# Five of nine gates and four adaLN vectors written between the blocks of an attention, in step with their size

## The chip, the cores and the metric

One core of one Trainium2 chip. The number is device time in microseconds (us) for one launch; lower is better. TensorE (PE) multiplies, with its weight loads shown as a row of their own (PEld); VectorE is DVE, ScalarE is ACT, GpSimd is POOL, SyncE is SP. SP and ACT issue most DMAs, POOL a few.

## What is computed

One layer of a hybrid decoder on 1024 prompt rows and 8 x 4 new rows (1056 columns in all, held transposed):

```
mod = silu(c) @ w_ada + b_ada                 # six vectors of 1024: sh1 sc1 g1 sh2 sc2 g2
h   = rmsnorm(x) * (1 + sc1) + sh1
z   = h @ w_in + b_in                         # q, k, v, forget, glu, gate_a, gate_b
o   = fox_attention(q, k, v, logf)            # 8 heads of 64, causal, with a forget bias
y_a = o @ w_pa
y_b = silu(layernorm(conv(glu))) @ w_pb + b_pb
x   = x + g1 * ((sigmoid(gate_a) * y_a + sigmoid(gate_b) * y_b) @ w_o)
x   = x + g2 * (swiglu(rmsnorm(x) * (1 + sc2) + sh2))
```

Arithmetic is float32 made of two float32r halves, so each product is three matmuls (high by high, high by low, low by high).

## The kernel before

The kernel is written as one long program, and a planner then orders it: it steps through a simulation of the chip, and whenever an engine is free it takes the earliest-written instruction that is ready in that simulation. Each engine executes the resulting list strictly in that order. `in_order(x)` adds one constraint: x may not be placed ahead of the instruction written just before it on the same engine. `tc.high_priority()` moves a block forward in the planner's ranking.

A **gate** (`gate_steps(i)`) is one 128-row slice of gate_a (i = 0 to 7) or gate_b (8 to 15) before its sigmoid: it loads a 512 KB weight tile on SP (L309, buffer tag `wr`, three buffers), splits it in high and low halves (ACT L315, POOL L318), and multiplies it with three column chunks of 384, 384 and 288, eight steps (k) of three matmuls (`mm3`, L327 to L329) each. After each chunk ACT copies the result out of PSUM (L486) and stores it in `gD`. The products take PSUM buffers of tag `mm`, of which there are two while the attention runs.

An **adaLN vector** (`ada(i)`) is one of the six slices of `mod`. It streams eight 512 KB tiles of `w_ada` through the same `wr` buffers (SP, L157), each used by four matmuls of 32 rows (L161) into one `mm` buffer; then come an ACT copy, two transposes (L170) and one DVE addition (L173). Vectors 2 to 5 are not needed before the layer's output products.

The **attention** has 32 units: head h by column block c2, in the order 3, 1, 2, 0 for each head. `scores` makes two blocks of 128 softmax rows: matmuls L815, L817, L818 into PSUM, DVE L820 to add the bias and find the minimum, DVE L825, ACT L826 for the exponential, DVE L827 and DVE or ACT for the division. `weighted` runs up to two units later: transposes L874, split into halves by ACT L876 and DVE L877, products with V L886 and L887, sum of two halves by ACT L897 and DVE L898, store from the ACT queue. `load_head` brings five operands of a head from HBM on SP (L849 to L853), two heads ahead. `conv_ln` (three times) normalises the convolution branch in between. Before the attention stand the gates 15 to 10; behind it, in the written order, gates 9, 8, 6, 5, 4, 3, 2, 1, 0, with the vectors 2 to 5 behind the gates 6, 5, 4 and 3. The planner takes these for the places where TensorE would be free during the attention. Then follow the convolution's product (`branch(1, ...)`, loads `yr` L941), gate 7, and the rest of the layer.

```
for n, u in enumerate(units):
    ready.append((*u, scores(*u)))
    if n in (0, 8, 16):
        conv_ln(n // 8)
    if len(ready) > 2:
        weighted(*ready.pop(0))
    if n % 4 == 1 and 4 < n < 28:
        load_head(n // 4 + 1)
for x in ready:
    weighted(*x)
for i in (9, 8, 6, 5, 4, 3, 2, 1, 0):
    gate(i, pool, sp)
    if 3 <= i < 7:
        ada(8 - i, wp, "wr", 3, ps_mm)
```

Of the kernel before, what the change touches and what calls it, by code (L numbers as in the profile page):

```python
# [29 lines left out]
KD = D // P  # L30
# [14 lines left out]
ON = 150  # L45
KS = 2
NHR = 8
HF = 2
UW = KL + NP + DB * (KL + DT)

# [36 lines left out]
def hybrid_step(ctx, tc, xT, cT, vec, bvf, con, stT, ptab, ptabr, kcT, vc, lfc, w_ada, w_in, w_vfa, w_vfb,  # L87
# [61 lines left out]
    act.activation(cTt, cTt, AF.Silu)  # L149
    wap = mkpool(name="wap", bufs=1, side="right")  # L150

    def ada(i, pl, tag, bufs, psum):

        ps = psum()
        for k in range(KD):
            w = pl.tile([P, KD, P], F32, name="wa", tag=tag, bufs=bufs).rearrange("p a b -> p (a b)")
            d = sp.dma_start(w, w_ada[k * P:(k + 1) * P, i * 1024:(i + 1) * 1024])  # L157
            if i < 2:
                in_order(d)
            for g in range(4):  # L160
                pe.matmul(ps[32 * g:32 * g + 32, :256], cTt[:, k, :], w[:, g * 256:(g + 1) * 256],  # L161
                          start=(k == 0), stop=(k == KD - 1))
        with tc.high_priority() if i < 2 else nullcontext():
            s = ev(wp, "gev", 4)
            d = act.copy(s[:, :256], ps[:, :256])
            if i == 1:
                in_order(d)
            pt = psum()
            for q in range(2):
                pe.transpose(pt[:, q * P:(q + 1) * P], s[:, q * P:(q + 1) * P], ident)  # L170
            src = pt[:, :256].rearrange("p (q g r) -> p g q r", q=2, g=4)[:, :, :, 0:9]
            b = V[:, V_ADA + i * 8:V_ADA + i * 8 + 8].rearrange("p (g q) -> p g q", g=4)
            dve.tensor_tensor(mod[:, i * 8:(i + 1) * 8, :].rearrange("p (g q) r -> p g q r", g=4),  # L173
                              src, b.unsqueeze(3).broadcast_to([P, 4, 2, 9]), OP.add)
            if i == 1:
                gains(0, V_RMS1, 8)

    def gains(i, vcol, sc):
        g = V[:, vcol:vcol + KD]
# [142 lines left out]
        with tc.high_priority():  # L322
            return split_w(*args, **kw)

    def mm3(ps, w, k, nk, xh, xl, n):
        wh, wl = w
        pe.matmul(ps[:, :n], wh[:, k, :], xh, start=(k == 0), stop=False)  # L327
        pe.matmul(ps[:, :n], wh[:, k, :], xl, start=False, stop=False)  # L328
        pe.matmul(ps[:, :n], wl[:, k, :], xh, start=False, stop=(k == nk - 1))  # L329

# [138 lines left out]

    gD = [[dram.tile([P, T], F32, name=f"gD{w}_{j}") for j in range(KD)] for w in range(2)]  # L470

    def gate_steps(i, *wq):

        which, j = divmod(i, KD)
        w = w_in_tile(16 + i, *wq)
        for c in range(3):
            o, n = CH[c]
            ps = ps_mm()
            ah, al = A[c]
            for k in range(KD):  # L480
                mm3(ps, w, k, KD, ah[:, k, :n], al[:, k, :n], n)
                if k < KD - 1:
                    yield
            t = ev(wp, "gev", 4)
            vcol = (V_BGA, V_BGB)[which] + j
            act.activation(t[:, :n], ps[:, :n], AF.Identity, bias=V[:, vcol:vcol + 1])  # L486
            act.dma_start(gD[which][j][:, o:o + n], t[:, :n])
            yield
# [410 lines left out]
        act.dma_start(oD[p][64 * h2:64 * h2 + 64, c2 * 256:(c2 + 1) * 256], ot)  # L899

    units = [(h, c2) for h in range(H) for c2 in (3, 1, 2, 0)]
    ready = []
    load_head(0)
    load_head(1)
    for n, u in enumerate(units):
        ready.append((*u, scores(*u)))
        if n in (0, 8, 16):
            conv_ln(n // 8)
        if len(ready) > 2:
            weighted(*ready.pop(0))  # L910
        if n % 4 == 1 and 4 < n < 28:
            load_head(n // 4 + 1)
    for x in ready:
        weighted(*x)
    for i in (9, 8, 6, 5, 4, 3, 2, 1, 0):
        gate(i, pool, sp)
        if 3 <= i < 7:
            ada(8 - i, wp, "wr", 3, ps_mm)
    gains(1, V_RMS2, 32)
    atl.release()  # L920
    atp.release()
# [487 lines left out]
```

## Time and profile before

| what | value |
|---|---|
| median of 3 runs | 1625.02 us (1624.96 to 1627.49) |
| the profiled execution | 1624.47 us, span of its instructions 1622.7 us |
| PE busy | 1562.2 us, 96% |
| PEld busy | 1474.2 us, 91% |
| DVE busy | 1060.4 us, 65% |
| ACT busy | 698.6 us, 43% |
| mean granted clock of TensorE | 0.989 |

Matmuls overlap in the records, so PE counts as busy as long as one is in flight; the weight loads beside it (PEld) thin out where the matmuls come less densely. The attention runs from about 406 to 671 us.

### The profile page before, as it was taken

To read this page: it belongs to the slowest core of one execution; us is meant where nothing else is said; L and a number is where in the kernel's file an instruction comes from. 1 tells how busy PE (TensorE), PEld (TensorE's weight loads), DVE (VectorE), ACT (ScalarE), POOL (GpSimd) and SP (SyncE) were. 2 spreads that over 40 slices of the span, in tenths; PEclk is the share of its full clock that TensorE was granted. 3 is DMA by queue.
4 is the path that set the end of the run, shared out by engine and by line. 5 is a ranking of instruction groups with operands and counts; after the bars stand their busy time and mean duration, and the time that the engine had idled before them with its cause. 6 is when DMAs were issued, how large, how long until landed. Compare 5 with 4: busy or idle time off the path is not lost.

```text
span 1622.7 us, 29627 instructions
## 1 busy us (share of the span) xinstructions
PE 1562.2 (96%) x11280; PEld 1474.2 (91%) x11280; DVE 1060.4 (65%) x2206; ACT 698.6 (43%) x1398; POOL 131.9 (8%) x102
## 2 busy tenths in 40 slices
PE   5999999999998989999999999999999999999997
PEld 3899978778977878999999999999999999999997
DVE  6943379999797867256659995555555596225644
ACT  4552212121376766444427653333333375224342
POOL 2121022341220101000000000000000000000000
PEclk9999999999999999999999999999999999999998
DMA  9196475877697774454554322222222257334552
GB/s 370 57 311 183 150 222 181 255 227 220 196 248 227 208 212 155 141 169 144 181 184 132 118 93 86 80 80 79 80 80 80 79 186 256 115 89 136 192 173 82
DMA packets 141424, 261.86 MB, mean 161 GB/s; under 512 B 24634, under 2 KB 81594, under 8 KB 140642
## 3 DMA queue, kind: packets, MB, share of 16 engines
q1 hardware_dynamic: 102802, 209.37, 41.4%
q10 hardware_dynamic: 36384, 43.01, 7.6%
q0 software_dynamic: 2096, 7.60, 1.5%
q8 instruction: 88, 1.44, 0.4%
q14 instruction: 54, 0.44, 0.1%
HBM read 206.44 MB, written 53.48 MB: 160 GB/s over the span
## 4 chain that ended last, share of the span: by engine, by line
PE 77%; DVE 11%; DMA 6%; ACT 2%; POOL 2%; issue 2%; SPq 1%; ACTq 0%; DVEq 0%; POOLq 0%
PE mm L1177 25%; PE mm L1278 16%; PE mm L329 8%; PE mm L327 8%; PE mm L328 8%; DVE acc L528 5%; DMA wa<-w_ada 2%; PE ptr L874 2%; POOL wl L318 1%; PE mm L561 1%; PE mm L560 1%; PE mm L562 1%; PE mm L161 1%; PE ppv L887 1%; PE ppv L886 1%
## 5 line engine op out<-in xcount | busy, mean ns | idle before, releaser
L327 PE MATMUL mm<-ah,wh 128*128 128x384 f32 (+2 forms) x768 | 252.0, 329 | 7.6 <-ACT ah L291 3.7
L1278 PE MATMUL mm<-f,wo 128*128 128x352 f32 x1584 | 256.8, 323 | 0.0
L1278 PEld LDWEIGHTS mm<-f,wo 128*128 128x128 f32 x1584 | 254.8, 188 | 0.0
L329 PE MATMUL mm<-ah,wl 128*128 128x384 f32 (+2 forms) x768 | 251.3, 328 | 2.6 <-POOL wl L318 2.6
L328 PE MATMUL mm<-al,wh 128*128 128x384 f32 (+2 forms) x768 | 251.8, 328 | 0.0
L1177 PE MATMUL mm<-c,wc 128*128 128x264 f32 x1776 | 235.7, 285 | 1.0 <-ACT wc L1134 0.5
L1177 PE MATMUL mm<-b,wc 128*128 128x264 f32 x1680 | 227.3, 286 | 3.5 <-DVE wc L1135 1.3
L1177 PEld LDWEIGHTS mm<-c,wc 128*128 128x128 f32 x1776 | 224.2, 188 | 2.0 <-ACT gev L1182 0.9
L1177 PEld LDWEIGHTS mm<-b,wc 128*128 128x128 f32 x1680 | 213.9, 189 | 5.1 <-ACT wc L1134 1.8
L528 DVE SCALAR_TENSOR_TENSOR acc<-u,vec,acc 128x1024 f32<-128x1024 f32 x120 | 171.4, 1450 | 1.2
L327 PEld LDWEIGHTS mm<-ah,wh 128*128 128x128 f32 x768 | 145.5, 190 | 17.1 <-issue 5.9
L328 PEld LDWEIGHTS mm<-al,wh 128*128 128x128 f32 x768 | 145.3, 189 | 11.3 <-issue 10.5
L1229 DVE TENSOR_TENSOR wo<-wr,wo 128x512 fp32r<-128x512 f32 x108 | 69.7, 647 | 129.9 <-ACT wo L1228 129.3
L329 PEld LDWEIGHTS mm<-ah,wl 128*128 128x128 f32 x768 | 145.5, 190 | 7.3 <-POOL wl L318 3.5
L1134 ACT CAST wc<-wr 128x512 fp32r<-128x512 f32 x144 | 88.6, 620 | 138.8 <-PE mm L1177 131.0
L1228 ACT CAST wo<-wr 128x512 fp32r<-128x512 f32 x108 | 63.2, 585 | 151.0 <-PE mm L1278 143.8
L1135 DVE TENSOR_TENSOR wc<-wr,wc 128x512 fp32r<-128x512 f32 x144 | 98.7, 691 | 35.6 <-ACT wc L1134 34.4
L318 POOL TENSOR_TENSOR wl<-wr,wh 128x1024 fp32r<-128x1024 f32 x27 | 87.6, 3249 | 319.7 <-ACT wh L315 280.3
L315 ACT CAST wh<-wr 128x1024 fp32r<-128x1024 f32 (+1 forms) x64 | 59.8, 940 | 91.0 <-PE mm L328 45.9
L327 PE MATMUL mm<-b,wh 128*128 128x264 f32 x256 | 72.7, 285 | 0.5 <-ACT wh L315 0.5
L329 PE MATMUL mm<-b,wl 128*128 128x264 f32 x256 | 72.1, 285 | 0.6 <-DVE wl L318 0.6
L328 PE MATMUL mm<-b,wh 128*128 128x264 f32 x256 | 72.4, 283 | 0.0
(293 smaller groups left out, 2665.4 us busy)
## 6 DMA issues: line engine op xcount, KB each, us to landing
wr<-w_fi SPq DMA_DIRECT2D x52, 512.0 KB
wa<-w_ada SPq DMA_DIRECT2D x48, 512.0 KB
wr<-w_fo SPq DMA_DIRECT2D x36, 512.0 KB
kt<-kcT SPq DMA_DIRECT2D x64, 256.0 KB
vt<-vc SPq DMA_DIRECT2D x64, 256.0 KB
hD<-h ACTq DMA_DIRECT2D x44, 264.0 KB
wr<-w_in SPq DMA_DIRECT2D x18, 512.0 KB
wr<-w_o SPq DMA_DIRECT2D x16, 512.0 KB
```

The lines of the kernel that those rows point to most:

```text
L315: d = act.copy(wh[:, r, :], raw[:, r, :])
L318: eng.tensor_tensor(wl[:, r, :], raw[:, r, :], wh[:, r, :].bitcast(F32), OP.subtract)
L327: pe.matmul(ps[:, :n], wh[:, k, :], xh, start=(k == 0), stop=False)
L328: pe.matmul(ps[:, :n], wh[:, k, :], xl, start=False, stop=False)
L329: pe.matmul(ps[:, :n], wl[:, k, :], xh, start=False, stop=(k == nk - 1))
L528: dve.scalar_tensor_tensor(a[:, :NP], u[:, j:j + NP], wv[:, j:j + 1], a[:, :NP], op0=OP.mult, op1=OP.add)
L1134: act.copy(w[:, 0, :n], raw)
L1135: dve.tensor_tensor(w[:, 1, :n], raw, w[:, 0, :n].bitcast(F32), OP.subtract)
L1177: pe.matmul(ps[:, :HS], w[i][:, r, k * P:(k + 1) * P], x[s][:, k, :], start=(new and k == 0 and j == 0), stop=(k == 3 and j == 2), skip_gr ...
L1228: act.copy(x[:, 0, :], raw)
L1229: dve.tensor_tensor(x[:, 1, :], raw, x[:, 0, :].bitcast(F32), OP.subtract)
L1278: pe.matmul(ps[e][:, :n], w[r][:, k * P:(k + 1) * P], f[x], start=(k0 + k + i == 0), stop=(k0 + k == HT - 1 and i == 2))
```

## The change

Gates 9, 8 and 6 are written ahead of the attention. Gates 5, 4, 3, 2, 1 and vectors 2 to 5 are cut into 136 steps (120 of one k of a gate, 16 of two tiles of a vector), which are written between the attention's blocks: after each `scores` and each `weighted`, as many as bring the share of steps written up to the share of the attention's cost written, where a block of c2 counts 4 * c2 + 3. Every quarter of the gate steps takes one vector's four steps with it, one after each of its first four fours. The first matmul of each chunk of these gates, and the second tile's matmuls of each vector step, are held behind what is written before them on TensorE. A vector's step loads two tiles and multiplies the later one first. Gate 0 is written behind the attention.

```diff
--- before.py
+++ after.py
@@ -45,6 +45,7 @@
 ON = 150
 KS = 2
 NHR = 8
+FILL = (5, 4, 3, 2, 1)
 HF = 2
 UW = KL + NP + DB * (KL + DT)
 
@@ -149,17 +150,39 @@
     act.activation(cTt, cTt, AF.Silu)
     wap = mkpool(name="wap", bufs=1, side="right")
 
-    def ada(i, pl, tag, bufs, psum):
+    def ada(*args):
+        for _ in ada_steps(*args):
+            pass
+
+    def ada_steps(i, pl, tag, bufs, psum):
 
         ps = psum()
-        for k in range(KD):
+
+        def load(k):
             w = pl.tile([P, KD, P], F32, name="wa", tag=tag, bufs=bufs).rearrange("p a b -> p (a b)")
             d = sp.dma_start(w, w_ada[k * P:(k + 1) * P, i * 1024:(i + 1) * 1024])
             if i < 2:
                 in_order(d)
+            return w
+
+        def product(k, w, first, last, pinned=False):
             for g in range(4):
-                pe.matmul(ps[32 * g:32 * g + 32, :256], cTt[:, k, :], w[:, g * 256:(g + 1) * 256],
-                          start=(k == 0), stop=(k == KD - 1))
+                mm = pe.matmul(ps[32 * g:32 * g + 32, :256], cTt[:, k, :], w[:, g * 256:(g + 1) * 256],
+                               start=first, stop=last)
+                if pinned:
+                    in_order(mm)
+
+        if i < 2:
+            for k in range(KD):
+                product(k, load(k), k == 0, k == KD - 1)
+        else:
+
+            for k in range(0, KD, 2):
+                w0, w1 = load(k), load(k + 1)
+                product(k + 1, w1, k == 0, False)
+                product(k, w0, False, k == KD - 2, True)
+                if k < KD - 2:
+                    yield
         with tc.high_priority() if i < 2 else nullcontext():
             s = ev(wp, "gev", 4)
             d = act.copy(s[:, :256], ps[:, :256])
@@ -174,6 +197,7 @@
                               src, b.unsqueeze(3).broadcast_to([P, 4, 2, 9]), OP.add)
             if i == 1:
                 gains(0, V_RMS1, 8)
+        yield
 
     def gains(i, vcol, sc):
         g = V[:, vcol:vcol + KD]
@@ -322,9 +346,11 @@
         with tc.high_priority():
             return split_w(*args, **kw)
 
-    def mm3(ps, w, k, nk, xh, xl, n):
+    def mm3(ps, w, k, nk, xh, xl, n, pinned=False):
         wh, wl = w
-        pe.matmul(ps[:, :n], wh[:, k, :], xh, start=(k == 0), stop=False)
+        first = pe.matmul(ps[:, :n], wh[:, k, :], xh, start=(k == 0), stop=False)
+        if pinned:
+            in_order(first)
         pe.matmul(ps[:, :n], wh[:, k, :], xl, start=False, stop=False)
         pe.matmul(ps[:, :n], wl[:, k, :], xh, start=False, stop=(k == nk - 1))
 
@@ -469,7 +495,8 @@
 
     gD = [[dram.tile([P, T], F32, name=f"gD{w}_{j}") for j in range(KD)] for w in range(2)]
 
-    def gate_steps(i, *wq):
+    def gate_steps(i, *wq, pinned=False):
+
 
         which, j = divmod(i, KD)
         w = w_in_tile(16 + i, *wq)
@@ -478,7 +505,7 @@
             ps = ps_mm()
             ah, al = A[c]
             for k in range(KD):
-                mm3(ps, w, k, KD, ah[:, k, :n], al[:, k, :n], n)
+                mm3(ps, w, k, KD, ah[:, k, :n], al[:, k, :n], n, pinned and k == 0)
                 if k < KD - 1:
                     yield
             t = ev(wp, "gev", 4)
@@ -899,23 +926,63 @@
         act.dma_start(oD[p][64 * h2:64 * h2 + 64, c2 * 256:(c2 + 1) * 256], ot)
 
     units = [(h, c2) for h in range(H) for c2 in (3, 1, 2, 0)]
+
+    def gate_fill():
+        for i in FILL:
+            yield from gate_steps(i, pool, sp, pinned=True)
+
+    def ada_fill():
+        for i in (2, 3, 4, 5):
+            yield from ada_steps(i, wp, "wr", 3, ps_mm)
+
+    def fillers():
+
+        gates, vectors = gate_fill(), ada_fill()
+        part = 3 * KD * len(FILL) // 4
+        for _ in range(4):
+            for n in range(part):
+                next(gates)
+                yield
+                if n % 4 == 3 and n < 16:
+                    next(vectors)
+                    yield
+        for _ in vectors:
+            pass
+
+
+    fill = fillers()
+    total = 3 * KD * len(FILL) + 16
+    blocks = 2 * sum(4 * c2 + 3 for _, c2 in units)
+    spent = filled = 0
+
+    def fill_up(c2):
+        nonlocal spent, filled
+        spent += 4 * c2 + 3
+        while filled < spent * total // blocks:
+            next(fill, None)
+            filled += 1
+
+    for i in (9, 8, 6):
+        gate(i, pool, sp)
     ready = []
     load_head(0)
     load_head(1)
     for n, u in enumerate(units):
         ready.append((*u, scores(*u)))
+        fill_up(u[1])
         if n in (0, 8, 16):
             conv_ln(n // 8)
         if len(ready) > 2:
-            weighted(*ready.pop(0))
+            weighted(*ready[0])
+            fill_up(ready.pop(0)[1])
         if n % 4 == 1 and 4 < n < 28:
             load_head(n // 4 + 1)
     for x in ready:
         weighted(*x)
-    for i in (9, 8, 6, 5, 4, 3, 2, 1, 0):
-        gate(i, pool, sp)
-        if 3 <= i < 7:
-            ada(8 - i, wp, "wr", 3, ps_mm)
+        fill_up(x[1])
+    for _ in fill:
+        pass
+    gate(0, pool, sp)
     gains(1, V_RMS2, 32)
     atl.release()
     atp.release()
```

## Rows read from the trace of the kernel before

**Rows 1.** The page: busy time, share of the span, instructions of each engine.
```profile
PE 1562.2 (96%) x11280; PEld 1474.2 (91%) x11280; DVE 1060.4 (65%) x2206; ACT 698.6 (43%) x1398; POOL 131.9 (8%) x102
```

**Rows 2.** Windows: start:end length; busy us (instructions) of PE, PEld, DVE, ACT, POOL; clock, DMA share, GB/s.
```profile
394.10:426.30 32.20, 31.68 (x193) 31.31 (x192) 28.52 (x26) 9.19 (x13) 8.67 (x3) 1.00 0.95 262
426.30:671.20 244.90, 230.44 (x1656) 199.56 (x1655) 178.25 (x566) 155.25 (x319) 31.69 (x27) 0.98 0.64 189
457.80:479.50 21.70, 20.08 (x153) 12.96 (x153) 18.69 (x61) 16.97 (x34) 3.15 (x4) 1.00 0.93 295
502.00:534.20 32.20, 27.59 (x207) 20.77 (x207) 24.50 (x84) 25.75 (x53) 3.59 (x4) 0.95 0.87 260
557.20:588.50 31.30, 27.18 (x198) 19.46 (x198) 20.85 (x72) 19.56 (x41) 0.70 (x1) 0.89 0.85 240
610.00:629.30 19.30, 18.92 (x165) 13.90 (x164) 14.96 (x50) 11.50 (x25) 0.83 (x1) 1.00 0.76 258
479.50:502.00 22.50, 22.06 (x155) 21.32 (x153) 20.45 (x65) 14.65 (x31) 5.41 (x6) 1.00 0.60 176
588.50:610.00 21.50, 19.91 (x134) 18.84 (x132) 14.61 (x42) 11.03 (x25) 1.66 (x1) 1.00 0.70 180
678.10:700.20 22.10, 20.05 (x113) 17.71 (x112) 11.12 (x16) 11.47 (x17) 0.00 (x0) 1.00 0.73 229
```

**Rows 3.** Groups by line, 390 to 690 us: xcount | busy, mean ns | idle before.
```profile
L886 PE MATMUL ppv<-pth,vh 128*128 128x256 f32 (+1 forms) x160 | 43.3, 291 | 0.5 <-DVE ot L898 0.5
...
L815 PE MATMUL pss<-k,q 128*128 128x512 f32 (+2 forms) x96 | 37.4, 389 | 0.5 <-DVE mx L820 0.5
...
L874 PE MATMUL ptr<-con,px 128*128 128x128 f32 x208 | 33.0, 278 | 4.7 <-DVE ptl L877 4.7
L161 PE MATMUL mm<-wa,cT 128*32 128x256 f32 x256 | 25.2, 405 | 5.4 <-DMA wa<-w_ada 5.4
L817 PE MATMUL pss<-maskr,identr 128*128 128x128 f32 x64 | 15.3, 240 | 0.0
L874 PE MATMUL ptr<-con,py 128*128 128x128 f32 x80 | 13.9, 287 | 0.0
...
L318 POOL TENSOR_TENSOR wl<-wr,wh 128x1024 fp32r<-128x1024 f32 x9 | 23.1, 2566 | 140.8 <-ACT wh L315 125.0 <-DMA oD<-ot 15.6
```

**Rows 4.** Timeline of PE, single matmuls: start us, us, what.
```profile
394.12 0.34 PE L327 MATMUL mm<-ah,wh 128*128 128x384 f32 x1
...
405.71 0.39 PE L815 MATMUL pss<-k,q 128*128 128x512 f32 x1
...
495.17 0.28 PE L886 MATMUL ppv<-pth,vh 128*128 128x256 f32 x1
495.29 0.28 PE L887 MATMUL ppv<-ptl,vh 128*128 128x256 f32 x1
...
495.76 0.39 PE L815 MATMUL pss<-k,q 128*128 128x512 f32 x1
495.99 0.40 PE L818 MATMUL pss<-kl,q 128*128 128x512 f32 x1
...
498.50 0.60 PE L874 MATMUL ptr<-con,px 128*128 128x128 f32 x4
498.85 0.38 PE L328 MATMUL mm<-al,wh 128*128 128x288 f32 x1
...
618.38 0.64 PE L161 MATMUL mm<-wa,cT 128*32 128x256 f32 x8
618.95 0.66 PE L874 MATMUL ptr<-con,px 128*128 128x128 f32 x4
```

**Rows 5.** Waits of all engines, 426 to 672 us: us in total, times, longest.
```profile
DVE px L820 <- PE pss L818: 11.2, 9, 4.3
...
PE mm L161 <- DMA wa<-w_ada: 5.4, 4, 2.6
```

**Rows 6.** Waits of the SP queue, 390 to 690 us: same columns.
```profile
SPq L157 <- PE mm L161: 42.2, 11, 11.9
```

## The prediction

> **What bounds the kernel now.** I read the page first. TensorE is busy for 96% of the span and its weight loads for 91%, VectorE for 65% [rows 1]: TensorE's stream of matmuls sets the time, and an edit that moves matmuls without removing any can win only where that stream is thin. So I then cut the part that the change touches into windows. Around 394 to 426 us it is dense: the weight loads fill 31.3 of 32.2 us. Over the attention, 426.3 to 671.2 us, they fill 199.6 of 244.9 us. The third to sixth windows of the group are those in which an adaLN vector is multiplied; there they fill 13.0 of 21.7, 20.8 of 32.2, 19.5 of 31.3 and 13.9 of 19.3 us, 64% together, and the granted clock falls to 0.95 and 0.89. The next two are windows in which a gate is multiplied: 21.3 of 22.5 and 18.8 of 21.5 us, 95% and 88% [rows 2]. The thin places are those where the planner has no gate at hand, because the vector's tiles sit in the three buffers through which the gates' weights come too. (The share of the weight loads is only a pointer, since small matmuls have short loads; the sum below counts matmuls.)
>
> **How much is lost there.** I price each matmul by its distance to the next start in a dense place [rows 4], and count from the groups [rows 3]. A gate: 405.71 - 394.12 = 11.6 us for its 72 matmuls. Scores: 0.23 us for 512 columns; the 8 heads have 8 x 2 x 4608 = 73,728 columns, 33.1 us, and 64 mask matmuls at a quarter of 0.23 are 3.7. V products: 0.12 us for 256 columns; by the loops again 73,728 columns, 34.6. Transposes: 0.35 for four, 288 of them, 25.2. Layernorm: some 40 small ones at about 0.1, 4. The attention's own stream is 100.6 us. A vector: 0.57 for eight matmuls, 64 of them, 4.6, and its two transposes 0.2; four vectors 19. From 394.1 to 678.1 us, where the last gate ends, ten gates run (10, 9, 8, 6, 5 to 0), so 116 + 100.6 + 19 = 235.6 us of work in 284.0. TensorE loses 48.4 us, some 47 of them inside the attention: 19% of its 244.9.
>
> **The change part by part.**
>
> *Gates 9, 8, 6 ahead.* No matmul is added. After gate 10 ends at 405.7, three gates take 34.8 us, to 440.5. Today one gate and a half run there, while VectorE, 28.5 of 32.2 us busy, finishes the convolution's sums [rows 2]. Their three 512 KB loads now stand ahead of the heads' loads on SP; two more of them are 1 MB, 4 us at the 262 GB/s of that window, and the scores that wait behind them are needed 35 us later than today, which covers it. Their splits on POOL, 2.6 us each [rows 3], hide beside 11.6 us of matmuls, and their stores go out on ACT's queue as before: nothing. What is queued behind them is the attention itself, and VectorE's share of it: that is the third rival.
>
> *Five gates and the vectors between the blocks.* The stage then holds 100.6 + 19 + 5 x 11.6 = 177.6 us of work on TensorE and the same 178.3 us on VectorE [rows 2]. Each is a lower bound, and neither is reached. From above: if VectorE stays at today's 178.3 of 244.9, 73%, the stage lasts 245 us. From below: at the best window's 20.5 of 22.5, 91%, 196 us [rows 2]. For TensorE, 19% lost gives 219 us, and the 5% of the better gate window 187. I take 215 us: TensorE then loses 17.4%, VectorE is 83% busy, halfway between its mean and its best. I don't go lower, because a chunk's later steps are free to be pulled ahead of their written place, so each chunk is spent in the first gaps behind its start, and because one of the two `mm` buffers is held by a vector while the gates share the other. I don't go higher, because VectorE waited 11.2 us for scores alone [rows 5], and such waits come from the same thin stretches.
>
> *Pairs of tiles.* The bytes are the same. Today's matmuls wait 5.4 us visibly for the tiles [rows 5], and SP stands 42.2 us in front of their loads until a buffer is free, with the heads' loads behind it [rows 6]. Spread over all the stage the pairs are 215/136 x 5 = 8 us apart while a vector runs, against 4 us for 1 MB at the 240 to 295 GB/s of those windows [rows 2]. I count the wait at nothing more than it is today; below, a saving of 5.4 us; above, the second rival. The slow clock is part of the 48.4 us: 5% of 32.2 and 11% of 31.3 us, 5 us in all [rows 2], at half speed (1.2 GHz instead of 2.4) behind pauses of TensorE.
> A rule speaks against this part. The Trainium skill (TensorE: Matmul & The Clock Gate, section "HAM oscillation — how this bites in real kernels") advises to run all contraction tiles of an output before the next wait for a load, because waits between them let the clock fall. The pairs do the reverse. Here the two falls came in windows without other matmuls at hand, and the pairs have gate steps and attention between them, so I don't add its price; by it, 16 falls of 1.6 us (the smaller of the two windows) instead of 5 us would be 21 us more.
>
> *Holds on the first matmul of a chunk.* They cost no time by themselves; behind the held one stands all of TensorE's later list, so if `weighted` before it is late, the gate is too. Priced within the 215 us.
>
> *Gate 0 behind.* 11.6 us after the attention's last product; today 6.9 us of gate work are left there (671.2 to 678.1). The next stage then loses at most 22.1 - 17.7 = 4.4 us, waiting for its first operands [rows 2]; 4.7 us more cover saves between nothing and 4.4, and I take 1.5. Gate 0 isn't held in place, so it may also slide forward, which is the lower end.
>
> *All else* (ACT's and VectorE's instructions, the later stages) is the same work in the same order; nothing.
>
> **The sum.** 440.5 + 215 + 11.6 = 667.1 against 678.1: 11.0 us less, and 1.5 behind it. The profiled execution took 1624.5 us (1.8 around its span) and lies 0.5 below the median; 1624.5 - 12.5 = 1612 us.
>
> **The rivals.**
>
> 1. *All of the starvation goes.* VectorE holds the 91% of its best window, the stage lasts 196 us: 19 us less, and with the 4.4 us behind it some 1590. For it: two windows at 86 and 91% [rows 2]. Against: none keeps that for more than 23 us, and the three windows after 557 us lie at 67 to 78%.
> 2. *Each pair waits for its load, and everything behind it.* TensorE takes its list in order, so a late tile holds scores, V products and gates alike. Today's four visible waits average 1.35 us; on 16 pairs that is 21.6 instead of 5.4 us, 1612 + 16 = 1628. It decides above 1.1 us a pair, where it eats the 12.5 us. For it: the vectors' windows already run at 0.76 to 0.93 of the DMA engines [rows 2]. Against: a wait per pair replaces one per tile, and there are 8 us between pairs. By the rule of the Trainium skill named above the pairs would end at 1612 + 21 = 1633.
> 3. *The attention keeps its own pace, and the result is slower.* If the chain of scores, minimum, exponential and turn sets the stage and not TensorE, the three gates in front delay it and gate 0 follows it: at 73% of VectorE 440.5 + 245 + 11.6 = 697 us, 1624.5 + 19 = 1643. It decides below 78%: 178.3 / (678.1 + 1.5 - 440.5 - 11.6). For it: in the window from 588.5 us a gate fills TensorE and VectorE is still only 14.6 of 21.5 us busy [rows 2]. Against: the waits on scores [rows 5].
> 4. *The change moves the loss and doesn't lessen it.* The planner already had nine gates to draw on, its picture of the chip is as wrong as before, and 48 us are lost in other places: 1623 to 1624.5. For it: the window from 588.5 us lost 12% with gates at hand. Against: 64% in the vectors' windows.
>
> **Chances.** The forecast (207 to 222 us for the stage, 1602 to 1619) 0.55; rival 1, 0.10; rival 2, 0.07; rival 3, 0.12; rival 4, 0.16, of which 0.03 still gains measurably. Within 0.2% (3 us) of 1625 is what a measurement of this kernel can't tell from no change. Faster: 0.55 + 0.10 + 0.03 = 0.68. Same: 0.13. Slower: 0.07 + 0.12 = 0.19. The range leaves out half of rival 1 below, and rival 3 from about 232 us and rival 2 with the full 1.35 us a pair and more above: 1597 to 1630. The likeliest case's own is 1602 to 1619.
>
> **What would show it.** In the windows of the attention: weight loads at 85% or more in every quarter, no stretch of 20 us near 64%; VectorE at 83%; the granted clock at 1.00 throughout; waits on the vectors' tiles under 6 us. The first score at about 440 us and the last product with V near 655. Wrong would be a VectorE under 78% with TensorE thin (rival 3), or visible waits of TensorE on w_ada of 15 us or more (rival 2).

## The result, and the profile after

The changed kernel takes 1640.74 us (median of 4 runs, 1638.67 to 1645.71), the kernel before 1624.99 us beside it (4 runs): a ratio of 1.0085, with a 95% interval of 1.0058 to 1.0111 (the ratios here and below are those on record; the two medians alone give 1.0097). It is slower, and 10.7 us above the range. The profiled execution took 1638.98 us with a span of 1637.2 us, 14.5 us more than before.

The page's line of busy times, as in [rows 1]:

```profile
PE 1566.8 (96%) x11280; PEld 1481.0 (90%) x11280; DVE 1066.8 (65%) x2206; ACT 698.7 (43%) x1398; POOL 131.7 (8%) x102
```

No instruction was added, and the shares don't show where the time went. The windows do, cut at the events that [rows 2] were cut at: the gates in front (to 443.5 us), the attention (to its last V product, 687 us) with four stretches inside it, the hole behind it, and the start of the convolution's product.

```profile
394.10:426.30 32.20, 32.20 (x199) 32.11 (x198) 30.67 (x29) 7.68 (x12) 7.76 (x3) 1.00 0.93 254
426.30:443.50 17.20, 17.20 (x110) 17.05 (x109) 3.99 (x5) 5.08 (x8) 5.38 (x4) 1.00 0.48 158
443.50:687.00 243.50, 223.43 (x1591) 193.53 (x1590) 179.19 (x562) 153.79 (x315) 27.02 (x23) 0.96 0.62 182
443.50:477.00 33.50, 32.22 (x245) 26.92 (x244) 27.61 (x84) 18.08 (x37) 5.68 (x4) 1.00 0.66 199
477.00:489.00 12.00, 9.05 (x46) 7.78 (x44) 7.79 (x28) 9.22 (x18) 3.02 (x3) 0.72 0.60 217
489.00:525.00 36.00, 34.25 (x264) 28.47 (x263) 30.92 (x106) 23.63 (x50) 3.65 (x5) 1.00 0.73 198
525.00:541.00 16.00, 9.43 (x37) 7.53 (x36) 9.68 (x25) 11.55 (x19) 2.36 (x1) 0.60 0.98 301
687.00:694.00 7.00, 0.45 (x4) 0.30 (x3) 0.44 (x2) 4.49 (x7) 0.00 (x0) 0.63 0.81 246
694.00:720.00 26.00, 25.85 (x140) 24.77 (x141) 14.04 (x19) 10.01 (x16) 0.00 (x0) 0.90 0.60 189
```

The reader is to see four things. The front is dense on TensorE, but VectorE, done with the convolution's sums, works 4.0 of 17.2 us there. The attention takes 243.5 us, as long as the 244.9 of [rows 2], with VectorE at 74% (73% before). Inside it are two thin stretches, 477 to 489 and 525 to 541 us, at clocks of 0.72 and 0.60. And from 687 to 694 us TensorE stands nearly still, where 6.9 us of gate work ran before. That last place stands in TensorE's timeline as follows (start, us, what, idle time before):

```profile
684.60 0.30 PE L355 MATMUL mm<-ah,wl 128*128 128x288 f32 x1
...
687.17 0.28 PE L914 MATMUL ppv<-ptl,vh 128*128 128x128 f32 x1
694.00 2.13 PE L351 MATMUL mm<-yh,wh 128*128 128x352 f32 x6 [6.55 <-ACT yh L1011]
```

The last gate's last matmul starts at 684.6 us, ahead of the last V products: gate 0, written behind the attention and not held, was drawn forward into it. Behind 687.2 us nothing is left to cover the 6.55 us until the next stage's first operand is split. The waits between 443.5 and 687 us (us in total, times, longest), which answer to [rows 5]:

```profile
ACT pth L903 <- PE ptr L901: 17.1, 20, 2.7
DVE ptl L904 <- ACT pth L903: 13.5, 17, 3.4
...
ACT wh L339 <- DMA wr<-w_in: 11.8, 4, 5.8
DVE px L847 <- PE pss L845: 10.1, 8, 6.6
...
PE ppv L913 <- ACT pth L903: 7.3, 3, 4.5
```

VectorE waits for scores about as long as before (10.1 us against 11.2). New is ACT's wait for the gates' weights, 11.8 us in four waits (0.7 us in one before); half of it lies in the second thin stretch, as ACT's timeline shows:

```profile
528.64 1.04 ACT L339 CAST wh<-wr 128x1024 fp32r<-128x1024 f32 x1 [5.82 <-DMA wr<-w_in]
```

The attention's casts stand behind that one in ACT's list. Both thin stretches also lie at the end of a `conv_ln`, for which ACT loads another function table and then goes back: three such loads of 1.28 us each fall between 525 and 541 us, one between 477 and 489. The attention of either kernel has eight of them, 10.3 us of ACT, so their number doesn't set the two apart; no run takes them out. The groups by line, 400 to 695 us, show TensorE's visible waits for the vectors' tiles at 3.7 us (5.4 in [rows 5]), and the SP queue's waits show their loads standing 48.7 us for a buffer (42.2 in [rows 6]):

```profile
L170 PE MATMUL mm<-wa,cT 128*32 128x256 f32 x256 | 22.2, 387 | 3.7 <-DMA wa<-w_ada 3.7
```
```profile
SPq L163 <- PE mm L170: 48.7, 15, 13.0
```

**Where the 14.5 us are.** The convolution's product starts at 694.0 us instead of 678.1, 15.9 us later, and what follows takes 943.2 instead of 944.5 us. Ahead of it the front ends 17.2 us later (443.5 against 426.3), the attention is 1.4 us shorter, and 7.0 us pass behind it where 6.9 passed before. In this profile, then, the gates in front were paid in full, and nothing came back for them. One count fits that: between the first V product and the last score both kernels start 316 gate matmuls. Behind the last score the kernel before starts 160 more, 45 of them behind the last V product, and the changed kernel 90, none of them behind it. The 70 that were moved, about one gate, were taken from the attention's end and not from its middle, where the planner had been spending gates all along. This says where the time stands; what each part of the change costs by itself is measured below.

### The profile page after: what moved, and what is told of

It reads as the page before. It is cut to its first block, busy times and chain, and to the rows that moved or that the text cites. A ratio compares the mean times of both kernels' runs of the same rounds, so it can differ in the third digit from the quotient of the medians.

```text
span 1637.2 us, 29631 instructions
## 1 busy us (share of the span) xinstructions
PE 1566.8 (96%) x11280; PEld 1481.0 (90%) x11280; DVE 1066.8 (65%) x2206; ACT 698.7 (43%) x1398; POOL 131.7 (8%) x102
## 4 chain that ended last, share of the span: by engine, by line
PE 67%; DMA 4%; DVE 4%; ACT 1%; issue 1%; SPq 0%; ACTq 0%; DVEq 0%
PE mm L1244 26%; PE mm L1345 16%; PE mm L351 6%; PE mm L355 6%; PE mm L354 6%; PE ptr L901 1%; DMA cvD<-xc 1%; DMA wr<-w_in 1%; PE mm L170 1%; PE pss L842 1%; PE ppv L914 1%; PE pss L845 1%; PE ppv L913 1%; DVE u L1081 1%; DMA wa<-w_ada 1%
## 5 line engine op out<-in xcount | busy, mean ns | idle before, releaser
L354 PEld LDWEIGHTS mm<-al,wh 128*128 128x128 f32 x768 | 145.7, 190 | 11.2 <-issue 10.4
L351 PE MATMUL mm<-b,wh 128*128 128x264 f32 x256 | 72.7, 285 | 0.5 <-ACT wh L339 0.5
```

The costliest lines, as they stand in the source:

```text
L351: first = pe.matmul(ps[:, :n], wh[:, k, :], xh, start=(k == 0), stop=False)
```

## The experiments

Two theories stood at first: rival 3 (the attention goes at its own pace, whatever lies between its blocks), and that what lies between its blocks lengthens it. Side theories were the weights that come late to ACT, the holds, and the last gate's place. All edits are of the changed kernel unless said. "Marks" are read in TensorE's timeline of each profiled execution: the first and the last V product, the first matmul of the convolution's product, and the time from there to the span's end. Each is read from one execution, and the runs of one kernel spread over some 7 us. Each edit also gives the planner another list, which it orders anew (one_pair_before has 473 gate matmuls between the first V product and the last score, where before has 316), so what follows prices an edit and its new order together.

| run | us | ratio to before (interval) | first V | last V | product | rest |
|---|---|---|---|---|---|---|
| before | 1624.99 | | 442.1 | 671.1 | 678.1 | 944.5 |
| after | 1640.74 | 1.0085 (1.0058–1.0111) | 455.6 | 687.2 | 694.0 | 943.2 |
| alone | 1698.12 | one run | 454.7 | 625.0 | 748.9 | 947.5 |
| gates_between | 1695.65 | one run | 460.0 | 652.4 | 737.6 | 956.3 |
| vectors_between | 1664.64 | one run | 458.8 | 653.2 | 715.5 | 947.4 |
| third | 1608.28 | one run | 458.8 | 661.5 | 664.4 | 941.8 |
| one_pair | 1628.64 | 1.0017 (1.0005–1.0029) | 459.9 | 676.8 | 683.9 | 941.8 |
| one_pair_before | 1630.94 | 1.0031 (1.0015–1.0047) | 446.7 | 684.8 | 687.9 | 943.0 |
| gate0_held | 1643.56 | 1.0104 (1.0071–1.0136) | 456.5 | 689.4 | 696.5 | 942.9 |
| gate0_behind | 1632.75 | 1.0054 (1.0033–1.0075) | 457.0 | 678.8 | 690.4 | 939.6 |
| front_only | 1632.40 | 1.0029 (1.0011–1.0048) | 454.5 | 685.4 | 688.4 | 942.6 |
| fill_eight | 1636.55 | 1.0063 (1.0044–1.0082) | 439.1 | 681.8 | 688.2 | 943.3 |
| no_holds | 1638.38 | 1.0082 (1.0057–1.0107) | 454.5 | 689.2 | 692.2 | 942.9 |
| low_rank | 1641.54 | 1.0098 (1.0078–1.0118) | 459.9 | 688.2 | 696.6 | 943.0 |
| even_spread | 1638.46 | 1.0073 (1.0044–1.0102) | 454.8 | 688.4 | 691.4 | 944.5 |
| pool_queue | 1647.18 | 1.0116 (1.0090–1.0141) | 460.7 | 698.9 | 704.9 | 944.9 |
| mixed_behind | 1631.24 | 1.0023 (1.0006–1.0039) | 446.7 | 680.7 | 683.5 | 942.1 |
| pairs_only | 1623.66 | 0.9983 (0.9967–0.9998) | 446.3 | 670.0 | 680.7 | 942.7 |
| pairs_again | 1623.17 | 0.9984 (0.9969–0.9999) | 444.6 | 666.9 | 677.6 | 941.8 |
| pairs_v5 | 1640.19 | 1.0082 (1.0061–1.0102) | 447.5 | 673.8 | 680.3 | 961.7 |

### Is it the attention's own pace?

**alone**: the three gates stand in front, the attention runs with nothing between, all the rest is held behind it.

```diff
     def fill_up(c2):
         nonlocal spent, filled
+        return
...
-                product(k + 1, w1, k == 0, False)
+                product(k + 1, w1, k == 0, False, True)
...
-    gate(0, pool, sp)
+    for _ in gate_steps(0, pool, sp, pinned=True):
+        pass
```

> The changed kernel with nothing written between the attention's blocks: the five gates, the four vectors and gate 0 all stand behind it, held there. Theory A (the attention's chain of scores, minimum, exponential and turn sets its own pace, whatever stands between): last score about 215 to 220 us after the front gates end, last V product about 240 us after, and then some 90 us of gates and vectors, so about 1700 us in all. Theory B (what was put between slows it: late weights, pairs, holds): last V product 190 to 200 us after the front gates, so about 1660 us.

The windows of the attention and of what is held behind it:

```profile
443.50:625.00 181.50, 146.51 (x905) 123.25 (x904) 160.49 (x554) 135.75 (x286) 14.68 (x18) 0.92 0.48 119
625.00:748.90 123.90, 95.34 (x652) 77.84 (x652) 8.84 (x13) 20.69 (x31) 11.83 (x5) 0.83 0.62 207
```

Alone the attention takes 181.5 us with VectorE 88% busy, 62 us less than with its fill: rival 3's mechanism falls, though its number, 1643 us, was nearly met. It is shorter even than the 190 to 200 us of theory B, while the total is nearly that of theory A: the total misleads here. The 384 gate matmuls between the last V product and the convolution's product need 62 us and the vectors 19, 81 us in all; they took 123.9 at a clock of 0.83. A reader of the 1698 us by itself would have said that the attention is slow by itself.

### What does each part of the fill cost?

**gates_between**: only the gates between the blocks, the vectors behind the attention. **vectors_between**: only the vectors, the gates behind. In both, what stands behind the attention is held there, and the last steps are written ahead of the last V products.

```diff
 # gates_between
-                if n % 4 == 3 and n < 16:
-                    next(vectors)
-                    yield
...
+    for _ in ada_fill():
+        pass
 # vectors_between
-                next(gates)
-                yield
-                if n % 4 == 3 and n < 16:
+                if n % 8 == 7 and n < 32:
                     next(vectors)
                     yield
...
+    for i in (*FILL, 0):
+        for _ in gate_steps(i, pool, sp, pinned=True):
+            pass
```

> The changed kernel with only the five gates between the blocks; vectors 2 to 5 and gate 0 held behind the last V product. From the end of the front gates to the last V product the attention took 181.5 us alone and 243.5 us with gates and vectors. Theory K (matmuls put between cost about 0.8 us each us, since VectorE is nearly full by itself and TensorE works its list in order): 58 us of gates give about 228 us. Theory L (the vectors' 16 MB of loads are what holds up): 190 to 205 us.

> The changed kernel with only the vectors between the blocks; gates 5 to 0 held behind the last V product. Theory K: 19 us of matmuls, the attention takes about 197 us. Theory L: 220 to 240 us.

**third**: two of the three matmuls of each step of the five gates are left out; their loads, splits and everything else stay.

```diff
+        if one:
+            return
         pe.matmul(ps[:, :n], wh[:, k, :], xl, ...
```

> The changed kernel with one of the three matmuls of each step of the five gates between (high by high alone, so these gates lack the two low products); all loads, splits, copies and stores stay. Theory K: 19 + 19 us of matmuls are left, about 212 us from the front gates to the last V product. Theory L: 235 to 244 us.

**one_pair** and **one_pair_before** (in the kernel before): six of the eight tiles of each of the vectors 2 to 5 aren't loaded; two tiles stand in for all (the cut is one_pair's).

```diff
-                w0, w1 = load(k), load(k + 1)
+                if k == 0:
+                    w0, w1 = load(k), load(k + 1)
```

> The changed kernel with six of the eight tiles of vectors 2 to 5 not loaded: the first pair is multiplied four times, so these four vectors are not the reference's. Matmuls, order and holds stay. Theory C: the buffers are free for the gates' weights, ACT's waits on them vanish and 10 to 16 us come back, 1624 to 1630 us. Theory D: 1635 to 1641 us.

> The kernel before with six of the eight tiles of vectors 2 to 5 not loaded (the first two are used four times; these vectors are not the reference's): the counterpart of the run that did this to the changed kernel and gained 10 to 12 us. Theory E (the vectors' 12 MB hold up any order): 1612 to 1618 us, so the loads explain nothing of the difference. Theory F (only the changed order is hurt by them): 1621 to 1628 us, and the difference between the two kernels is mostly gone without these loads.

The attention's windows from 443.5 us to the last V product, in the order gates_between, vectors_between, third, one_pair (one fence for each kernel):

```profile
443.50:652.40 208.90, 191.33 (x1281) 175.05 (x1279) 174.70 (x554) 145.21 (x304) 24.50 (x22) 0.98 0.47 128
```
```profile
443.50:653.20 209.70, 166.23 (x1191) 133.83 (x1190) 167.30 (x562) 139.25 (x293) 19.98 (x20) 0.91 0.67 190
```
```profile
443.50:661.50 218.00, 191.23 (x1384) 161.30 (x1383) 172.06 (x562) 152.60 (x318) 27.02 (x23) 0.95 0.72 208
```
```profile
443.50:676.80 233.30, 222.47 (x1608) 194.17 (x1606) 176.84 (x562) 153.60 (x315) 26.69 (x23) 0.98 0.49 137
```

The first V product doesn't mark the start of the fill: 51 of the 360 gate matmuls of gates_between stand ahead of it, and 48 of the 256 vector matmuls of vectors_between. So the stretches are taken from the front's last gate matmul, which starts at 444.4 us in alone, 446.4 in gates_between, 446.9 in vectors_between, 444.6 in gate0_behind (below), 443.2 in after, 447.8 in third and 445.1 in one_pair. From there to the last V product alone takes 180.7 us. Five gates (58 us of matmuls) add 25.3, the four vectors (19 us of matmuls) 25.6, and both with gate 0 held behind 53.5: a little more than their sum. A microsecond of gate work costs 0.44, one of a vector 1.35. Theory K had 228 us for gates_between, 197 for vectors_between and 212 for third, theory L 190 to 205, 220 to 240 and 235 to 244; the windows show 208.9, 209.7 and 218.0, so neither holds, and third comes nearest to K.

Behind the attention the price is another: in gates_between 85 us pass from the last V product to the product's start, at a clock of 0.53, for the four vectors and next to no gate matmuls (gate 0 slid behind that start, and the rest takes 956.3 us), 21 us a vector. Of the vectors' price about half is their loads: without six of eight tiles the same stretch of the changed kernel falls from 244.0 to 231.7 us, and the DMA share from 0.62 to 0.49. The count of TensorE's matmuls matters too: third leaves out 2/3 of 58 = 38.7 us of them and the stretch falls to 213.7, by 30.3, 0.78 each and not the 0.44 of gates_between. Neither the loads nor the matmuls are therefore free, even where both TensorE and VectorE have gaps. Without the loads the two orders come to the same (1628.64 and 1630.94). The kernel before got slower without them, which neither theory of one_pair_before foresaw; its last gate matmul starts at 657.5 us and its last V product at 684.8, so its end stood uncovered. That this made it slower is argued, not shown.

### The parts of the change one by one

**front_only** (kernel before, with gates 9, 8, 6 ahead of the attention, and vector 2 still ahead of gate 5), **fill_eight** (no gates in front, eight between), **pairs_only** (the order of before, the vectors by pairs), and **no_holds**:

```diff
 # front_only, against before
+    for i in (9, 8, 6):
+        gate(i, pool, sp)
     ready = []
     load_head(0)
...
-    for i in (9, 8, 6, 5, 4, 3, 2, 1, 0):
+    ada(2, wp, "wr", 3, ps_mm)
+    for i in (5, 4, 3, 2, 1, 0):
 # fill_eight
-FILL = (5, 4, 3, 2, 1)
+FILL = (9, 8, 6, 5, 4, 3, 2, 1)
-    for i in (9, 8, 6):
-        gate(i, pool, sp)
 # pairs_only
+        return    # first line of fill_up's body
...
-    for i in (9, 8, 6):
-        gate(i, pool, sp)
...
+    for i in (9, 8, 6, 5, 4, 3, 2, 1, 0):
+        gate(i, pool, sp)
+        if 3 <= i < 7:
+            ada(8 - i, wp, "wr", 3, ps_mm)
 # no_holds
-            yield from gate_steps(i, pool, sp, pinned=True)
+            yield from gate_steps(i, pool, sp)
-                product(k, w0, False, k == KD - 2, True)
+                product(k, w0, False, k == KD - 2)
```

> The kernel before with one edit: gates 9, 8 and 6 in front of the attention (vector 2 stays ahead of gate 5). Theory A (front gates delay the attention one for one, 17 us, and its pace does not change): 1638 to 1643 us, as the whole change. Theory B (the slowdown is made by the pairs, the holds and the mixing): 1622 to 1628 us.

> The changed kernel with no gate in front: FILL is 9, 8, 6, 5, 4, 3, 2, 1, all between the blocks, vectors by pairs as before. Theory A (the front gates are the loss): back to 1621 to 1628 us. Theory B (the mixing is the loss, and there is now more of it): 1638 us or more.

> The kernel before with the vectors by pairs of tiles as the only edit; all gates and vectors written behind the attention as they were. Theory C: the pairs bring the late weights with them, 1631 to 1637 us. Theory D: nothing, 1622 to 1628 us.

> The changed kernel without any hold: the gates' chunks and the vectors' second tiles may be taken as early as the planner likes. Theory C (late weights: pairs sit in two of the three buffers, gate weights come late, and ACT stands in its queue in front of their split, 11.8 us in all, with the attention behind it): 1637 to 1642 us, no change. Theory D (the place in the order: held and high-ranked gate steps go ahead of scores and VectorE, which needs 178 us for the attention by itself, runs dry): 1628 to 1634 us.

By the ratios the front alone makes the kernel 4.7 us slower, the mixing without the front 10 us, and the pairs alone make it 2.8 us faster. front_only and fill_eight each fell between their two theories: neither part is the whole loss. Leaving out the holds changes nothing: the ratio is 1.0082, and the planner starts its last gate matmul at 656.5 us. Only the pairs are worth keeping. They also wait more for the tiles than the changed kernel does (waits from 426.3 to 670 us):

```profile
PE mm L170 <- DMA wa<-w_ada: 15.7, 8, 5.0
```

and are the fastest complete version all the same. 15.7 us is what the prediction had named as proof of rival 2; as proof it was no good. **pairs_again** repeats the same kernel on another chip:

> The kernel before with the vectors by pairs as the only edit, a second time and in more rounds. If its first result (0.9983, interval 0.9967 to 0.9998) was more than chance: 1622 to 1624.5 us beside 1626 for the kernel before. If the pairs are worth nothing by themselves: a ratio of 0.999 to 1.001.

0.9984 against 0.9983: the gain is small, and holds. **pairs_v5** moves vector 5 out of it, behind gate 7 in the stage that follows:

```diff
-        if 3 <= i < 7:
+        if 4 <= i < 7:
...
     gate(7, dve, sp)
+    ada(5, wp, "wr", 3, ps_mm)
```

> The same with vector 5, which is needed only at the last residual, written behind gate 7, after the attention. Put between the blocks the four vectors lengthened the attention by 24 us for 19 us of matmuls, so one of them by about 6 us. If the same holds in the order before: 6 us off the attention, 4.6 us of matmuls later, and some wait for its tiles there, 1619 to 1624 us. If the attention hides a vector written behind it: 1626 to 1630 us.

This fell. The product starts as early as in pairs_only (680.3 us), but the rest takes 961.7 us, 19.0 more (17.0 by the medians of pairs_v5 and pairs_again), and the windows show the place:

```profile
700.00:730.00 30.00, 30.00 (x187) 30.00 (x186) 13.47 (x23) 12.82 (x25) 0.00 (x0) 1.00 0.55 170
730.00:760.00 30.00, 20.60 (x149) 15.84 (x148) 4.60 (x5) 4.67 (x8) 0.00 (x0) 0.77 0.49 163
```

A vector with no other matmuls at hand costs about four times its 4.6 us of matmuls. The price of 25.6 / 4 = 6.4 us that vectors_between gives was seen between the attention's blocks alone.

### The last gate, the late weights, the order

**gate0_held** holds each step of gate 0 at its written place; **gate0_behind** also writes the last chunks of fill ahead of the last group of V products, so that gate 0 truly stands behind them.

```diff
 # gate0_held
-    gate(0, pool, sp)
+    for _ in gate_steps(0, pool, sp, pinned=True):
+        pass
 # gate0_behind, with it
-    for x in ready:
+    for x in ready[:-1]:
         weighted(*x)
         fill_up(x[1])
+    fill_up(ready[-1][1])
     for _ in fill:
         pass
+    weighted(*ready[-1])
```

> The changed kernel with gate 0's chunks held behind the attention. Theory A (the tail of V products is a chain of its own, 24 us, and the 7 us hole behind it is what gate 0 should have covered): the hole closes, but gate 0's 11.6 us move behind the last V product; 1636 to 1642 us unless the tail gets shorter without the gate. Theory B (gate 0 in the tail slows it): the last V product comes 8 us earlier, 1632 us.

> The changed kernel with gate 0 really behind the last V product (the last fill steps are written ahead of the last weighted block, and gate 0's first matmul is held behind it; in the earlier attempt it was held behind a gate step that itself lay in the attention). If the 7 us hole ahead of the convolution's product is only missing cover: the hole goes, the last V product comes up to 8 us earlier, 1632 to 1638 us. If the tail's length is its own chain: the 11.6 us come on top of it less the hole, 1640 to 1645 us.

gate0_held came out above both of its theories: its last gate matmul still starts at 686.9 us, ahead of the last V product at 689.4. A hold only keeps an instruction behind those before it, and here that was a fill step which itself lay among the V products. gate0_behind does what the change says it does (windows of the attention, of gate 0 and of the product's start):

```profile
443.50:678.80 235.30, 212.71 (x1532) 182.38 (x1530) 177.22 (x561) 151.49 (x311) 26.87 (x23) 0.97 0.63 185
678.80:690.40 11.60, 11.60 (x75) 11.60 (x74) 2.85 (x3) 3.84 (x6) 0.00 (x0) 1.00 0.55 175
690.40:720.00 29.60, 29.34 (x182) 29.05 (x180) 14.16 (x22) 14.52 (x26) 0.00 (x0) 1.00 0.69 220
```

Gate 0 takes its 11.60 us at full density, the product starts with no hole, and the rest is 939.6 us, 3.6 less than after. By the ratios it ends 5 us below the changed kernel (8 by the medians) and still 9 above the kernel before.

Four edits went at the late weights of the gates and at the order: **low_rank** gives the fill a lower priority in the planner, **even_spread** takes a vector's pair after every seventh gate step, **pool_queue** loads the gates' weights from POOL's queue instead of SP's, **mixed_behind** gives the planner all nine gates, unheld, with the vectors' pairs spread among them, behind the attention as before.

```diff
 # low_rank
+        with tc.high_priority(offset=-3000):
+            while filled < spent * total // blocks:
 # even_spread
-                if n % 4 == 3 and n < 16:
+                if n % 7 == 6:
 # pool_queue
-            yield from gate_steps(i, pool, sp, pinned=True)
+            yield from gate_steps(i, pool, pool, pinned=True)
 # mixed_behind, with fill_up empty and nothing in front
+FILL = (9, 8, 6, 5, 4, 3, 2, 1, 0)
-                if n % 4 == 3 and n < 16:
+                if n % 13 == 12:
```

> The changed kernel with the steps between the blocks ranked far behind (3000 places) in the planner's choice; place in the text, holds and pairs stay. Theory C: 1637 to 1642 us. Theory D: scores go first again, VectorE's share of the stage rises above 78%, 1625 to 1631 us.

> The changed kernel with each vector's four steps spread over its whole quarter (one behind every seventh gate step) and not over the first sixteen. Theory C (bunched loads make gate weights and head loads late): ACT's waits on gate weights halve, 1628 to 1634 us. Otherwise 1636 to 1642 us.

> The changed kernel with one edit: the five gates between the blocks fetch their weights through POOL's queue and not through SP's, where the vectors' loads stand waiting for buffers. Theory G (the weights come late because SP stands still ahead of them): ACT's 11.8 us of waits on them vanish, 1628 to 1633 us. Theory H (they come late because the buffers or the DMA engines are full): waits stay, 1636 to 1643 us.

> Gates 9, 8, 6, 5 to 0 and the vectors' pairs mixed as in the change (a pair behind every 13th gate step), but all written behind the attention and without holds, for the planner to take forward. If the thin stretches of the kernel before come only from vectors without gates beside them, 1610 to 1618 us. If mixing brings late gate weights wherever it stands, 1628 to 1640 us.

None helps enough. In even_spread ACT's wait for the gates' weights is down from 11.8 to 2.6 us and the kernel takes 1638.46 us: the late weights make a thin stretch, but not the lost time. pool_queue, slower than both of its theories, still has 8.4 us of them and moves TensorE's waits for the vectors' tiles to 13.6 us. low_rank changes nothing. mixed_behind is 3.7 us slower than before by its ratio, and pairs_only, which leaves the planner whole vectors and whole gates, beats it.

## Why the prediction was wrong

By its own steps, with 667.1 us forecast for the product's start and 694.0 measured, 26.9 us more (each measured term is from one execution, so the small ones are rough):

- **Gates 9, 8, 6 ahead**: 440.5 us forecast, 443.5 measured, +3.0. The size was nearly right. The first score, which the text expected at about 440 us, starts at 410.85: the planner drew four of the score matmuls over `k` ahead of 443.5 us. For the rest of the second softmax block VectorE waits 6.6 us, for a score matmul that stands behind the front's last gate matmul. What the step left out is that VectorE has 13.2 of the front's last 17.2 us to spare, while its 179 us of work in the attention stay.
- **Five gates and the vectors between the blocks**: this step failed. The stage was put at 215 us on the reading that TensorE starves and that matmuls at hand would fill its gaps, so that it loses 17.4% and VectorE is 83% busy. With exactly this fill, gate0_behind takes 235.3 us from the same mark, VectorE 75% busy: +20.3. The thin stretches were taken for lack of gates; the attention alone has 181.5 - 100.6 = 81 us of gaps, but a gate put there costs 0.44 of its time and a vector more than all of it. That VectorE is 88% busy when nothing lies between, and 75% with the fill, shows that TensorE's work at hand was not what it lacked. The upper bound, 245 us, was named, and the value was set between the bounds with nothing that measured it. The kernel before had a pointer that was only weighed: in its window from 588.5 us a gate filled TensorE and the rate of the attention fell (VectorE 68% busy) [rows 2].
- **Gate 0 behind**: a wrong mechanism. The caveat that it might slide forward was priced as the lower end, a gain; it was a loss, 3.6 us (243.5 + 7.0 in the changed kernel against 235.3 + 11.6 in gate0_behind) and as much again in the rest behind it. 3.0 + 20.3 + 3.6 is the 26.9. The ratios put gate 0's place at 5 us in all.
- **Behind it**: 1.5 us less forecast, 1.3 less measured, but not for the cover, which is missing: the first 26 us behind the hole run at a clock of 0.90, and only gate0_behind, with cover, goes 4.9 us below before.
- **Pairs of tiles**: right that they cost nothing, and the only part that pays: visible waits of 3.7 us in the changed kernel, and a ratio of 0.998 when they are the only edit. The Trainium skill's rule (TensorE: Matmul & The Clock Gate, section "HAM oscillation — how this bites in real kernels"), by which the split would have cost 21 us, doesn't decide here: with other matmuls beside the pairs no run shows such a loss. Where pairs stood by themselves the clock did fall, to 0.53 behind the attention in gates_between and to 0.77 in the window of pairs_v5, but no run has unsplit vectors there to compare. Where the clock fell in the changed kernel, in the two thin stretches, TensorE stood for turned blocks from ACT and not for the vectors' tiles; the second lies behind the late weight and ACT's table loads.
- **Holds**: right, nothing (no_holds, 1.0082 against 1.0085).
- **Rivals**: 1 and 2 fell. Rival 3 came within 3 us of the time by another mechanism. It said that 73% of VectorE is the attention's pace, and alone it runs at 88%. The sign that the text set for it, VectorE under 78% with TensorE thin, was there, and proves no more than the waits on the tiles do. Rival 4, that the loss only moves, describes the sum of front and attention best, but it stopped at no change; it didn't count that the moved gates were what had stood at the attention's end.

**Open.** The runs give the price of the fill and not all of its mechanism. Loads and matmuls were each seen to matter (one_pair, third), and the price isn't proportional to either. What `conv_ln` and its table loads cost the attention wasn't tried, nor what a plan at the chip's true prices would give.

## What to carry to other kernels

A gap on TensorE in a stage that another engine paces is not room: measure the stage without its fill, and price each kind of fill by the time that it adds between two marks, before counting on the gap. Read such a run by its marks and not by its total, because what is moved out runs at another price in its new place. Work that is moved ahead of a stage is taken away from its end, so look at what covers the next stage's first operands, and whether the planner will leave it there.

## What the runs showed of the hardware that wasn't expected

A gate's split on POOL can hold up a VectorE instruction for as long as it runs. Between alone and gates_between VectorE's instructions in the attention are the same 554, but it is 174.7 instead of 160.5 us busy. The timelines of gates_between show where, VectorE's and then POOL's:

```profile
466.61 2.53 DVE L852 SCALAR_TENSOR_TENSOR st<-mx,Cq 128x1 f32<-128x1 f32 x2
```
```profile
466.75 2.37 POOL L342 TENSOR_TENSOR wl<-wr,wh 128x1024 fp32r<-128x1024 f32 x1 [10.92 <-ACT wh L339]
```

The second of the two, an instruction over one column that takes 0.24 us on average in alone, lasts as long as the split. Beside each of the four splits in that stretch one VectorE instruction takes 2.40 to 2.61 us: two of one column and two of 288 columns, which take 0.3 and 0.5 us elsewhere, some 8.6 us too long in all. Three of the five splits in the changed kernel have one of 2.29 to 2.44 us. The kernel before has it too: this one-column instruction averages 0.34 us in its attention. Not every instruction waits: in third, beside the split from 472.70 to 475.09 us, VectorE's five instructions that read PSUM, or one column, take their usual 0.15 to 0.74 us. The Trainium skill (SBUF — State Buffer, section "SBUF: two separate sides") says that the two engines share a pair of ports as an exclusive lock, which a VectorE instruction needs in some modes or when it has two inputs in SBUF, and that whichever starts second is blocked for all of the other's instruction; the trace agrees, with 2.4 us for the instruction over one column, both of whose inputs lie in SBUF. How much of the attention's 25 us for five gates this makes is not shown: the 8.6 us are argued from the durations and weren't tried by themselves.

A vector's 4.6 us of matmuls took 19 to 21 us where nothing else was at hand (pairs_v5, with a clock of 0.77, and gates_between, with 0.53), against 6.4 us between the attention's blocks.
